# Attention masks in a two-layer decoder trunk: from bf16 matmuls into the score banks to an add inside the row-maximum instruction

## The chip, the cores and the metric

The kernel runs on one core of one Trainium2 chip. The time is in device microseconds (us), from the first to the last instruction of one execution as the device counts it; three runs of the kernel before gave a median of 985.11 us (984.95 to 986.36). Everything else below is read from one further execution that the hardware profiler recorded. The engines are TensorE (PE for its matmuls, PEld for its weight loads), VectorE (DVE), ScalarE (ACT), GpSimd (POOL) and the transfer queues.

## The reference

A layer has three attention branches over 256 tokens of width 1024, merged by gates, then a feed-forward part and a per-layer gate; there are two layers. What matters here is the attention:

```python
def masked_softmax(scores, mask):
    p = jax.nn.softmax(jnp.where(mask, scores, NEG_INF), axis=-1)
    return jnp.where(mask, p, 0.0)
# A: selected blocks and a window, both causal for 256 tokens, gated per head
# B: window of 128 keys (a band), with a learned sink per head:
sink = jnp.broadcast_to(sinks...)
p = jax.nn.softmax(jnp.concatenate([s, sink], axis=-1), axis=-1)[..., :-1]
# C: causal, latent attention, 8 heads of 96
```

Each branch has 8 heads. A also has a branch over 15 compressed keys, whose mask the change leaves as it is.

## The kernel before, in words

**Weights.** All weights are streamed once from HBM in chunks of two 128-row tiles by 512 columns. ScalarE rounds a chunk to its upper part (`wh`) and VectorE subtracts to get the lower part (`wl`). `lin` (line 316) multiplies 256 tokens by a weight matrix as three products of parts into a bank of PSUM, one bank per 128 tokens; the tile name of these banks is `lin`. Four raw chunks and six split chunks fit.

**Units of attention.** A unit is one bank of scores: 128 query rows, 512 columns. For the first 128 tokens (t = 0) a bank holds four row groups of 128 keys, for the second (t = 1) two of 256 keys. A layer has 24 such units: C has 2 with t = 0 and 4 with t = 1, A has 4 (`sw`, t = 0) and 8 (`sel` and `win`, t = 1), B has 2 and 4. Two units over compressed keys (`cmp`) come besides. Over two layers there are 48 units, 16 with four groups and 32 with two.

**The steps of a unit.** `qk` (line 859) first writes the mask into the bank by one bf16 matmul of the identity (`identb`) with `masks` (line 874): 512 columns for t = 0 and for B, else only the upper 256. The score matmuls then add to it (line 886; 4 to 8 of them). VectorE takes the negated maxima of the rows in one instruction (line 891, `negm`). For B three small instructions follow, which bring in the sink (lines 895 to 897). `ex` (line 899) has ScalarE take the exponential of each group, out of PSUM, with `negm` as the bias and with the row sum; `nrm` (line 912) inverts the sums on VectorE and scales `p`; `tr` (line 926) transposes `p` on TensorE and ScalarE copies the result (`pT`); `pvm` (line 938) multiplies with the values into a bank `pv`; after the last unit of a branch and t, `fin` (line 965) splits the output into `oT`. The tile `p` (three buffers, shared with a few other tiles) is taken in `ex`.

**The order.** Each engine runs its instructions in the order in which they are written. The class `Plan` (line 68) keeps an estimate of each engine's time from shapes alone; every step is queued with the time at which its operands are expected and is written between the matmuls of `lin` when the estimate of TensorE's time passes it (`tick`, line 139, after every three matmuls). A new unit is written (`hook`, line 848) when its inputs are there, fewer than two units wait for their exponential, and the estimate of TensorE's time is at least `SPACE` = 4.4 past that of the last unit. Where the main stream needs a result (`branch`, line 1093: branch C's products `wc0` need both of C's `oT`, `wb0` needs B's), `until` (line 151) writes all that is still queued up to it first.

**Once.** `setup_masks` (line 397) makes the bf16 identity, the rounded identity and the bf16 masks on VectorE. The arithmetic of the inverse roots (`newton`) is a chain of small instructions on POOL.

Of the kernel before, what the change touches and what calls it, by code (L numbers as in the profile page):

```python
# [10 lines left out]
BF16 = mybir.dt.bfloat16  # L11
I32 = mybir.dt.int32
AF = mybir.ActivationFunctionType
ALU = mybir.AluOpType
# [12 lines left out]
# The weight stream of a layer, in the order of use: name, k-tiles, columns, k-tiles of a chunk.  # L27
# [29 lines left out]
# columns of the constants, in three parts  # L57
# [3 lines left out]
# columns of a layer's small parameters  # L61
# [6 lines left out]
class Plan:  # L68
    """An estimate of when each engine's work ends, from shapes alone. Each engine runs its instructions in
    the order of emission, so a step that waits for another engine is put between the main stream's matmuls  # L70
    at the place where its operands are expected."""
# [19 lines left out]
    def clear(self, key, bufs):  # L91
        """Emit what still reads the slot's tile."""
        h = self.slots.setdefault(key, [])
        if len(h) >= bufs:
            for n in range(100):
                held = [x for x in self.q if h[-bufs] in x[3]]
                if not held:
                    break
                x = min(held, key=lambda x: x[:2])
                self.q.remove(x)  # L100
                was, self.busy = self.busy, True
                x[2]()
                self.busy = was
# [26 lines left out]
    def push(self, aps, fn, more=0.2, holds=()):  # L130
        """Emit fn when aps are expected; it reads the tiles of aps and holds."""
        self.n += 1
        self.q.append((max(self.at(*aps) + more, self.now), self.n, fn, {a.tensor.name for a in (*aps, *holds)}))
# [37 lines left out]
class Engine:  # L171
    """An engine whose instructions are entered into the plan."""
# [37 lines left out]
def build(tc, wst, xin, pin, posn, cst, lpar, fnorm, out):  # L210
# [39 lines left out]
    def upper(i):  # L250
        """Chunk i's upper parts."""
        for j in sorted(late):
            if j <= i - RAWB:
                late[j]()
        load_to(i + 1)
        off, kk, c = CHUNKS[i]
        r = raws.pop(i)
        hi = sb([P, 1024], F32R, name="wh", bufs=HLB, p=wp)
        lo = sb([P, 1024], F32R, name="wl", bufs=HLB, p=wp)
        w = kk * c  # L260
        S.copy(out=hi[:, :w], in_=r[:, :w])
        hls[i] = (hi, lo)

        def rest():
            late.pop(i)
            V.tensor_tensor(out=lo[:, :w], in0=r[:, :w], in1=hi[:, :w].bitcast(F32), op=ALU.subtract)
            load_to(i + 1 + RAWB)
        late[i] = rest

    def feed():  # L270
        """Split the next chunks where the engines have time."""
# [44 lines left out]
    def lin(l, name, nk, lhs, evac, blocks=None, wait=0.0, halves=False):  # L316
        """psum[tok, cols] = sum over k of lhs(t, k) x weights, three products of float32r parts."""
# [68 lines left out]
    identb = sb([P, P], BF16, name="identb")  # L386
    identr = sb([P, P], F32R, name="identr")
    masks = sb([P, 2, P], BF16, name="masks")
# [8 lines left out]
    def setup_masks():  # L397
        V.tensor_copy(out=identb, in_=ident)
        V.tensor_copy(out=identr, in_=ident)
        W.push([mload], lambda: V.tensor_copy(out=masks, in_=mload))  # L400
# [59 lines left out]
    def newton(ssq, n, tag, G=G):  # L460
        """(ssq + eps) ** -0.5 for [128, n]; a second term of ssq may be added."""
# [20 lines left out]
    def split_evac(src_ps, n, hi, lo, then, gain=None):  # L482
        """PSUM [128, n, 128] (times a gain per partition and n) -> parts."""
# [14 lines left out]
    def finish(t, r):  # L498
        """The final norm: x * gain lies in xf."""
# [11 lines left out]
    class Norm:  # L511
        """RMSNorm of x: transposed parts of x * gain; the inverse root goes into the products' outputs."""
# [16 lines left out]
        def square(self, t, g, c=slice(0, 512), part=0):  # L529
            """The sum of squares over columns c of half g, divided by D; the last norm also takes x * gain."""  # L530
# [54 lines left out]
    def rope(src, n, h, tab, dst):  # L585
        """src [128, n, 2h] -> dst; tab [128, 4h] = cos cos sin sin."""
# [8 lines left out]
    def layer(l, nm, nxt):  # L595
# [9 lines left out]
        # slots of 8 KB that the layer's stages share  # L605
# [41 lines left out]
        dup = [[None, None], [None, None]]  # L647
        vS = [sb([P, 3, P], name=f"v{t}") for t in range(2)]
# [210 lines left out]
        def qk(u):  # L859
# [5 lines left out]
            if t == 0:  # L865
                m = masks[:, 1:2, :].to_broadcast([P, 4, P])
                o = b.rearrange("p (a b) -> p a b", a=4)
            elif kind == "b":
                m = masks[:, None, :, :].to_broadcast([P, 2, 2, P])
                o = b.rearrange("p (c a b) -> p c a b", c=2, a=2)  # L870
            else:
                m = masks[:, 1:2, :].to_broadcast([P, 2, P])
                o = b.rearrange("p (c a b) -> p c a b", c=2, a=2)[:, :, 1, :]
            T.matmul(out=o, lhsT=identb, rhs=m, start=True, stop=True)
            for n, j in enumerate(js):
# [9 lines left out]
                for rk in rks:  # L885
                    T.matmul(out=b[:, n * w:(n + 1) * w], lhsT=lq, rhs=rk, start=False, stop=True,
                             skip_group_check=True)
            hs = slice(4 * c + js[0], 4 * c + js[0] + nh)
            b3 = b.rearrange("p (a b) -> p a b", a=ng)
            negm = small(4, "negm", 3)[:, :ng]  # L890
            V.tensor_reduce(out=negm, in_=b3, axis=AXX, op=ALU.max, negate=True)
            if v == "B":
                sk = lp[:, L_SINK:L_SINK + 8][:, hs]
                ns = small(4, "ns", 3)[:, :nh]
                V.tensor_scalar(out=ns, in0=sk, scalar1=-1.0, scalar2=None, op0=ALU.mult)
                V.tensor_tensor(out=negm, in0=negm, in1=ns, op=ALU.min)
                V.tensor_tensor(out=ns, in0=sk, in1=negm, op=ALU.add)

            def ex():
                p = sb([P, 512], name="p", bufs=3)  # L900
                state["open"] -= 1
                sm = small(4, "sm", 3)[:, :ng]
                for h in range(ng):
                    S.activation(out=p[:, h * nk:(h + 1) * nk], in_=b[:, h * nk:(h + 1) * nk], func=AF.Exp,
                                 bias=negm[:, h:h + 1], scale=1.0, accum_out=sm[:, h:h + 1])
# [70 lines left out]
            W.push([ns if v == "B" else negm], ex, 0.2, [b, negm])  # L976

        def qk_cmp(u):
# [18 lines left out]
            def nrm():  # L997
                V.tensor_reduce(out=m, in_=s, axis=AXX, op=ALU.add)
                V.reciprocal(out=m, in_=m)
                # gates lie as (c, j), the heads here as (j, c)  # L1000
# [266 lines left out]
    def warm(n):  # L1267
        """Keep the tensor engine's clock up until the first data are there."""
        for _ in range(n):
            nc.tensor.matmul(out=wps, lhsT=wrm[:, 0:P], rhs=wrm, start=True, stop=True)  # L1270
# [72 lines left out]
def host_layout(inputs):  # L1343
    """Weights in the order of use, chunk by chunk; small parameters along partitions."""
# [87 lines left out]
```

## Time and profile before

| | |
|---|---|
| median of three runs | 985.11 us |
| profiled execution, first to last instruction | 984.9 us |
| PE, busy | 967.0 us, 4915 matmuls |
| PEld, busy | 786.1 us |
| DVE, busy | 669.2 us, 1070 instructions |
| ACT, busy | 556.2 us, 1013 instructions |
| POOL, busy | 105.4 us, 224 instructions |

The page gives the span of the profiled execution and no other time of it; the median of the runs is 0.2 us above that span. Matmuls overlap in the records, because each is shown until its result is there; what one costs is read from the distance of two starts, and the same holds for two VectorE instructions in a row.

### The profile page before, as it was taken

To read this page: it belongs to the slowest core of one execution; us is meant where nothing else is said; L and a number is where in the kernel's file an instruction comes from. 1 tells how busy PE (TensorE), PEld (TensorE's weight loads), DVE (VectorE), ACT (ScalarE), POOL (GpSimd) and SP (SyncE) were. 2 spreads that over 40 slices of the span, in tenths; PEclk is the share of its full clock that TensorE was granted. 3 is DMA by queue.
4 is the path that set the end of the run, shared out by engine and by line. 5 is a ranking of instruction groups with operands and counts; after the bars stand their busy time and mean duration, and the time that the engine had idled before them with its cause. 6 is when DMAs were issued, how large, how long until landed. Compare 5 with 4: busy or idle time off the path is not lost.

```text
span 984.9 us, 13708 instructions
## 1 busy us (share of the span) xinstructions
PE 967.0 (98%) x4915; PEld 786.1 (80%) x4915; DVE 669.2 (68%) x1070; ACT 556.2 (56%) x1013; POOL 105.4 (11%) x224
## 2 busy tenths in 40 slices
PE   8899999999999999999999999999999999999996
PEld 5688887777888888888878898877778888888885
DVE  4687688658776666645767868876786766565555
ACT  5567766665555444543556686666655544444443
POOL 6610000000030000000444000000001200000032
PEclk9999999999999999999999999999999999999999
DMA  7445624434455555555454654343344555555551
GB/s 260 161 158 195 220 93 148 149 108 138 168 182 184 191 190 187 176 184 195 149 177 146 197 200 160 115 164 128 129 142 159 195 191 188 186 180 192 176 167 43
DMA packets 46596, 164.29 MB, mean 167 GB/s; under 512 B 5504, under 2 KB 5760, under 8 KB 46528
## 3 DMA queue, kind: packets, MB, share of 16 engines
q1 hardware_dynamic: 45648, 161.80, 48.7%
q0 software_dynamic: 448, 1.30, 0.4%
q8 instruction: 39, 0.64, 0.3%
q10 hardware_dynamic: 432, 0.32, 0.1%
q14 instruction: 29, 0.24, 0.1%
HBM read 162.35 MB, written 1.05 MB: 166 GB/s over the span
## 4 chain that ended last, share of the span: by engine, by line
PE 93%; POOL 3%; DVE 1%; issue 1%; ACT 1%; ACTq 0%; POOLq 0%; DVEq 0%
PE lin L206 78%; PE tr L206 6%; PE sc L206 5%; PE pv L206 3%; PE hidps L206 2%; POOL n1a L206 0%; POOL n0a L206 0%; POOL ang L206 0%; POOL kq L206 0%; ACT wh L206 0%; POOL kp L206 0%; DVE um L206 0%; DVE wl L206 0%; POOL n0y L206 0%; POOL n0v L206 0%
## 5 line engine op out<-in xcount | busy, mean ns | idle before, releaser
L206 PE MATMUL lin<-wh,hT 128*128 128x512 f32 (+2 forms) x1600 | 516.9, 392 | 1.5 <-DVE hT L206 0.8
L206 DVE TENSOR_TENSOR wl<-raw,wh 128x1024 fp32r<-128x1024 f32 (+2 forms) x308 | 369.1, 1209 | 94.6 <-ACT wh L206 89.5
L206 ACT CAST wh<-raw 128x1024 fp32r<-128x1024 f32 (+2 forms) x308 | 317.3, 1038 | 138.8 <-PE lin L206 135.7
L206 PEld LDWEIGHTS lin<-wh,hT 128*128 128x128 f32 x1600 | 297.9, 189 | 61.8 <-DVE hT L206 1.7
L206 PE MATMUL lin<-wl,hT 128*128 128x512 f32 (+2 forms) x800 | 308.1, 385 | 2.3 <-DVE wl L206 2.3
L206 PEld LDWEIGHTS lin<-wl,hT 128*128 128x128 f32 x800 | 151.1, 189 | 29.7 <-DVE wl L206 3.1
L206 PE MATMUL lin<-wh,hd 128*128 128x512 f32 x352 | 112.6, 397 | 0.0
L206 PEld LDWEIGHTS lin<-wh,hd 128*128 128x128 f32 x352 | 66.2, 188 | 15.2
L206 POOL TENSOR_SCALAR n0v<-ssq 128x1 f32<-128x1 f32 x7 | 2.5, 358 | 694.1 <-ACT junk L206 694.1
L206 PE MATMUL lin<-wl,hd 128*128 128x512 f32 x176 | 69.4, 394 | 0.0
L206 PE MATMUL lin<-wh,oT 128*128 128x512 f32 x192 | 64.7, 398 | 0.0
L206 ACT ACTIVATE th<-lin,rh 128x256 f32<-128x256 f32 (+1 forms) x52 | 26.3, 505 | 67.8 <-PE lin L206 67.7
L206 ACT ACTIVATE p<-sc,negm 128x256 f32<-128x256 f32 (+1 forms) x128 | 52.7, 427 | 2.7 <-DVE negm L206 2.7
L206 DVE SCALAR_TENSOR_TENSOR th<-th,lin 128x256 f32<-128x256 f32 x44 | 18.4, 418 | 50.6 <-ACT th L206 50.6
L206 DVE TENSOR_REDUCE negm<-sc 128x2 f32<-128x512 f32 (+1 forms) x48 | 33.0, 688 | 27.9 <-PE sc L206 27.5
L206 ACT COPY pT<-tr 128x512 f32<-128x512 f32 x48 | 28.1, 585 | 36.8 <-PE tr L206 36.5
L206 PEld LDWEIGHTS lin<-wh,oT 128*128 128x128 f32 x192 | 36.0, 188 | 7.9 <-issue 0.8
L206 PE MATMUL lin<-wh,mT 128*128 128x512 f32 x128 | 42.0, 399 | 0.0
L206 PEld LDWEIGHTS lin<-wl,hd 128*128 128x128 f32 x176 | 33.1, 188 | 7.5
L206 PE MATMUL lin<-wl,oT 128*128 128x512 f32 x96 | 37.6, 392 | 0.0
L206 ACT CAST hd<-tr 128x256 fp32r<-128x256 f32 x44 | 16.3, 370 | 33.8 <-PE tr L206 33.8
L206 DVE TENSOR_TENSOR p<-p,sm 128x512 f32<-128x512 f32 x48 | 33.2, 692 | 2.1
(226 smaller groups left out, 1073.3 us busy)
## 6 DMA issues: line engine op xcount, KB each, us to landing
raw<-wst SPq DMA_DIRECT2D x296, 512.0 KB, 4.0
raw<-wst SPq DMA_DIRECT2D x8, 312.0 KB, 2.8
raw<-wst SPq DMA_DIRECT2D x4, 384.0 KB, 3.0
x<-xin SPq DMA_DIRECT2D x4, 256.0 KB, 6.0
w<-lpar POOLq DMA_DIRECT2D x2, 256.0 KB, 3.2
pr<-pin POOLq DMA_DIRECT2D x2, 256.0 KB, 3.3
fn<-fnorm SPq DMA_DIRECT2D x1, 512.0 KB, 3.1
out<-xf SPq DMA_DIRECT2D x2, 256.0 KB, 2.1
```

The source lines that it names most:

```text
L206: return fn(*a, **k)
```

## The change

- The mask matmuls go, with `identb` and the bf16 masks. The first score matmul of a group now starts its part of the bank and the last one ends it.
- `masks` becomes float32, four blocks of 128 columns: band, causal, zeros, causal. A t = 0 unit takes the last block, a t = 1 unit of B the first two, the other t = 1 units the zeros and the causal block. GpSimd writes the zeros, ScalarE copies the others, in two instructions.
- The one row-maximum instruction of a unit becomes one `tensor_tensor_reduce` per group (four for t = 0, two for t = 1). It reads the scores from PSUM and the mask from SBUF, writes p = -(score + mask) to SBUF over the whole group, and puts the smallest of these and of a start value in `negm`. The start value is the negated sink for B, else 3e38.
- The negated sinks of a layer (`nsk`) are made once on GpSimd as the layer begins. Of B's three small VectorE instructions in each unit one is left.
- The exponential is taken in place from p in SBUF, with scale -1.0.
- `p` is now taken in `qk`, and the queue of the plan holds `p` where it held the bank.

The diff, cut to these places (it also drops comments):

```diff
-    identb = sb([P, P], BF16, name="identb")
     identr = sb([P, P], F32R, name="identr")
-    masks = sb([P, 2, P], BF16, name="masks")
+    masks = sb([P, 4, P], name="masks")
...
     def setup_masks():
-        V.tensor_copy(out=identb, in_=ident)
         V.tensor_copy(out=identr, in_=ident)
-        W.push([mload], lambda: V.tensor_copy(out=masks, in_=mload))
+        G.memset(masks[:, 2:3, :], 0.0)
+        W.push([mload], lambda: S.copy(out=masks[:, 0:2, :], in_=mload))
+        W.push([mload], lambda: S.copy(out=masks[:, 3:4, :], in_=mload[:, 1:2, :]))
...
+        nsk = small(8, "nsk", 1)
+        G.tensor_scalar(out=nsk, in0=lp[:, L_SINK:L_SINK + 8], scalar1=-1.0, scalar2=None, op0=ALU.mult)
...
-            T.matmul(out=o, lhsT=identb, rhs=m, start=True, stop=True)
...
-                for rk in rks:
-                    T.matmul(out=b[:, n * w:(n + 1) * w], lhsT=lq, rhs=rk, start=False, stop=True,
-                             skip_group_check=True)
+                for i, rk in enumerate(rks):
+                    T.matmul(out=b[:, n * w:(n + 1) * w], lhsT=lq, rhs=rk, start=i == 0,
+                             stop=i == len(rks) - 1, skip_group_check=True)
...
-            V.tensor_reduce(out=negm, in_=b3, axis=AXX, op=ALU.max, negate=True)
+            m = masks[:, 3, :] if t == 0 else masks[:, 0:2, :] if kind == "b" else masks[:, 2:4, :]
+            p = sb([P, 512], name="p", bufs=3)
+            for h in range(ng):
+                r = slice(h * nk, (h + 1) * nk)
+                i1 = m if t == 0 else m.rearrange("p a b -> p (a b)")
+                V.tensor_tensor_reduce(out=p[:, r], in0=b[:, r], in1=i1, scale=-1.0,
+                                       scalar=nsk[:, hs][:, h:h + 1] if v == "B" else 3e38,
+                                       op0=ALU.add, op1=ALU.min, accum_out=negm[:, h:h + 1])
             if v == "B":
-                sk = lp[:, L_SINK:L_SINK + 8][:, hs]
                 ns = small(4, "ns", 3)[:, :nh]
-                V.tensor_scalar(out=ns, in0=sk, scalar1=-1.0, scalar2=None, op0=ALU.mult)
-                V.tensor_tensor(out=negm, in0=negm, in1=ns, op=ALU.min)
-                V.tensor_tensor(out=ns, in0=sk, in1=negm, op=ALU.add)
+                V.tensor_tensor(out=ns, in0=lp[:, L_SINK:L_SINK + 8][:, hs], in1=negm, op=ALU.add)
...
-                p = sb([P, 512], name="p", bufs=3)
...
-                    S.activation(out=p[:, h * nk:(h + 1) * nk], in_=b[:, h * nk:(h + 1) * nk], func=AF.Exp,
-                                 bias=negm[:, h:h + 1], scale=1.0, accum_out=sm[:, h:h + 1])
+                    S.activation(out=p[:, h * nk:(h + 1) * nk], in_=p[:, h * nk:(h + 1) * nk], func=AF.Exp,
+                                 bias=negm[:, h:h + 1], scale=-1.0, accum_out=sm[:, h:h + 1])
...
-            W.push([ns if v == "B" else negm], ex, 0.2, [b, negm])
+            W.push([ns if v == "B" else negm], ex, 0.2, [p, negm])
```

## Rows read from the trace of the kernel before

All instructions are written by helpers on line 206, so rows are told apart by their tiles.

**Rows 1.** The page: busy time of each engine with its share of the span and its instructions, and the shares of the chain that ended last by engine.

```profile
PE 967.0 (98%) x4915; PEld 786.1 (80%) x4915; DVE 669.2 (68%) x1070; ACT 556.2 (56%) x1013; POOL 105.4 (11%) x224
...
PE 93%; POOL 3%; DVE 1%; issue 1%; ACT 1%; ACTq 0%; POOLq 0%; DVEq 0%
```

**Rows 2.** Busy time in stretches: from and to, length, then PE, PEld, DVE, ACT and POOL busy with their instructions, granted clock, DMA share, GB/s. The first two are the attention of layer 0 and of layer 1, the third a part of the first.

```profile
101.00:240.00 139.00, 138.50 (x838) 111.22 (x838) 103.89 (x204) 91.33 (x230) 0.64 (x1) 1.00 0.42 141
582.00:719.00 137.00, 136.50 (x826) 109.95 (x825) 102.70 (x203) 89.94 (x228) 0.61 (x1) 1.00 0.41 141
...
140.00:160.00 20.00, 20.00 (x114) 16.12 (x114) 18.27 (x36) 13.65 (x46) 0.00 (x0) 1.00 0.33 111
```

**Rows 3.** Groups of instructions, shapes kept apart: the mask matmuls (count, then busy us, mean ns of one, idle before).

```profile
L206 PE MATMUL sc<-masks,identb 128*128 128x512 bf16 x24 | 9.3, 387 | 0.0
...
L206 PE MATMUL sc<-masks,identb 128*128 128x256 bf16 x24 | 6.7, 278 | 0.0
```

**Rows 4.** Timeline of PE at two units of C: start, length, instruction. A mask of 512 columns and the score matmul behind it, then one of 256 columns and the one behind it.

```profile
106.49 0.39 PE L206 MATMUL sc<-masks,identb 128*128 128x512 bf16 x1
106.72 1.06 PE L206 MATMUL sc<-kTC,qTC 96*128 96x128 f32 x8
...
111.60 0.27 PE L206 MATMUL sc<-masks,identb 128*128 128x256 bf16 x1
111.71 1.03 PE L206 MATMUL sc<-kTC,qTC 96*128 96x256 f32 x4
```

**Rows 5.** Groups by shape on DVE and ACT: the row maxima, the nearest two-operand instructions of 256 and 128 columns, the read of ScalarE's accumulator, and a ScalarE cast of 256 columns out of PSUM and out of SBUF.

```profile
L206 DVE TENSOR_REDUCE negm<-sc 128x2 f32<-128x512 f32 x32 | 22.0, 688 | 16.2 <-PE sc L206 15.9
...
L206 DVE TENSOR_REDUCE negm<-sc 128x4 f32<-128x512 f32 x16 | 11.0, 686 | 11.6 <-PE sc L206 11.6
...
L206 DVE TENSOR_TENSOR hd<-tr,hd 128x256 fp32r<-128x256 f32 x44 | 18.6, 422 | 10.0 <-ACT hd L206 10.0
...
L206 DVE TENSOR_TENSOR cs_s<-cs_s,cs_m 128x128 f32<-128x128 f32 x8 | 2.3, 292 | 0.3
...
L206 ACT ACTIVATION_READ_ACCUMULATOR p<-sc,negm 128x1 f32 x128 | 26.9, 210 | 0.0
...
L206 ACT CAST hd<-tr 128x256 fp32r<-128x256 f32 x44 | 16.3, 370 | 33.8 <-PE tr L206 33.8
...
L206 ACT CAST q<-kall 128x256 fp32r<-128x256 f32 x16 | 5.7, 405 | 15.3 <-DVE kall L206 15.3
```

**Rows 6.** Timeline, instructions that stand back to back on one engine: two of 256 columns and a row maximum on DVE, two small ones of a B unit on DVE, and two exponentials of 128 columns on ACT (the accumulator's read between them is left out).

```profile
142.32 0.76 DVE L206 TENSOR_TENSOR kall<-ra,rb 128x256 f32<-128x256 f32 x2
142.99 0.68 DVE L206 TENSOR_REDUCE negm<-sc 128x4 f32<-128x512 f32 x1
143.59 2.35 DVE L206 TENSOR_TENSOR wl<-raw,wh 128x1024 fp32r<-128x1024 f32 x2
...
144.74 0.36 ACT L206 ACTIVATE p<-sc,negm 128x128 f32<-128x128 f32 x1
...
145.09 0.35 ACT L206 ACTIVATE p<-sc,negm 128x128 f32<-128x128 f32 x1
...
204.06 0.16 DVE L206 TENSOR_SCALAR ns<-lp 128x4 f32<-128x4 f32 x1
204.25 0.16 DVE L206 TENSOR_TENSOR negm<-negm,ns 128x4 f32<-128x4 f32 x1
```

**Rows 7.** Timeline of layer 0 where branch C ends: the last unit's scaling on DVE, its transposes, the split of C's output, and the first matmul of `wc0`.

```profile
134.35 0.69 DVE L206 TENSOR_TENSOR p<-p,sm 128x512 f32<-128x512 f32 x1
...
135.40 0.60 PE L206 MATMUL tr<-con,p 128*128 128x128 f32 x4
...
140.40 0.69 DVE L206 TENSOR_TENSOR oT<-pv,oT 128x512 fp32r<-128x512 f32 x1 [1.78 <-ACT oT L206]
...
141.23 0.39 PE L206 MATMUL lin<-wh,oT 128*128 128x512 f32 x1
```

**Rows 8.** The same where branch B ends: the last unit's mask, its scaling, transposes, the cast of the output, and the matmuls in which `wa1` ends and `wb0` begins (the second of the two).

```profile
230.29 0.39 PE L206 MATMUL sc<-masks,identb 128*128 128x512 bf16 x1
...
236.03 0.69 DVE L206 TENSOR_TENSOR p<-p,sm 128x512 f32<-128x512 f32 x1
...
237.49 0.60 PE L206 MATMUL tr<-con,p 128*128 128x128 f32 x4
...
240.54 0.59 ACT L206 CAST oT<-pv 128x512 fp32r<-128x512 f32 x1 [0.67 <-PE pv L206]
...
241.00 0.62 PE L206 MATMUL lin<-wh,oT 128*128 128x512 f32 x2
```

**Rows 9.** Timeline of PE: the masks of two units of A that follow one another.

```profile
186.68 0.27 PE L206 MATMUL sc<-masks,identb 128*128 128x256 bf16 x1
...
191.91 0.28 PE L206 MATMUL sc<-masks,identb 128*128 128x256 bf16 x1
```

**Rows 10.** Timeline of the start: the making of the identity and the masks on DVE, PE's wait for a lower part behind them, and ScalarE's wait before its second gate.

```profile
25.16 0.22 DVE L206 CAST identb<-con 128x128 bf16<-128x128 f32 x1
...
25.43 0.29 DVE L206 CAST masks<-mload 128x256 bf16<-128x256 f32 x1
...
26.91 0.50 PE L206 MATMUL lin<-wl,hT 128*128 128x512 f32 x1 [1.12 <-DVE wl L206]
...
31.48 0.69 ACT L206 ACTIVATE gateC<-lin,rh 128x512 f32<-128x512 f32 x1 [3.51 <-POOL rh L206]
```

More of the change, by code (lines that the diff above doesn't have):

```diff
@@ L864, in qk @@
             ng = 512 // nk
[L865 to L873, printed above, removed]
-            T.matmul(out=o, lhsT=identb, rhs=m, start=True, stop=True)
             for n, j in enumerate(js):
@@ L884, in qk @@
                 w = 512 // nh
-                for rk in rks:
-                    T.matmul(out=b[:, n * w:(n + 1) * w], lhsT=lq, rhs=rk, start=False, stop=True,
-                             skip_group_check=True)
+                for i, rk in enumerate(rks):
+                    T.matmul(out=b[:, n * w:(n + 1) * w], lhsT=lq, rhs=rk, start=i == 0,
+                             stop=i == len(rks) - 1, skip_group_check=True)
             hs = slice(4 * c + js[0], 4 * c + js[0] + nh)
-            b3 = b.rearrange("p (a b) -> p a b", a=ng)
             negm = small(4, "negm", 3)[:, :ng]
-            V.tensor_reduce(out=negm, in_=b3, axis=AXX, op=ALU.max, negate=True)
+            m = masks[:, 3, :] if t == 0 else masks[:, 0:2, :] if kind == "b" else masks[:, 2:4, :]
[6 more added lines that the diff above has]
+                                       op0=ALU.add, op1=ALU.min, accum_out=negm[:, h:h + 1])
             if v == "B":
-                sk = lp[:, L_SINK:L_SINK + 8][:, hs]
                 ns = small(4, "ns", 3)[:, :nh]
-                V.tensor_scalar(out=ns, in0=sk, scalar1=-1.0, scalar2=None, op0=ALU.mult)
-                V.tensor_tensor(out=negm, in0=negm, in1=ns, op=ALU.min)
-                V.tensor_tensor(out=ns, in0=sk, in1=negm, op=ALU.add)
+                V.tensor_tensor(out=ns, in0=lp[:, L_SINK:L_SINK + 8][:, hs], in1=negm, op=ALU.add)
             def ex():
-                p = sb([P, 512], name="p", bufs=3)
                 state["open"] -= 1
```

## The prediction

> **What bounds the kernel now.** I read the page's busy times and the chain that ended last, then busy time by stretches for the two attention stages, then the distances of starts in the timeline. TensorE is busy for 98% of the span and makes 93% of the chain [rows 1]. In layer 0's attention it is busy for 138.5 of 139 us, in layer 1's for 136.5 of 137 [rows 2]: it waits for nobody there, so in these stages each us that it is spared would be worth a us, as long as the engines that feed it keep up. VectorE, which gets the work, is busy for 103.9 of 139 us, 75%, but unevenly: 18.27 of 20 us where branch A's first units meet the products of C [rows 2]. There it is as good as full. ScalarE has 91 of 139.
>
> **Removed from TensorE.** A mask of 512 columns holds the next matmul off by 106.72 - 106.49 = 0.23 us, one of 256 columns by 111.71 - 111.60 = 0.11 [rows 4]. There are 24 of each [rows 3]: 24 x 0.23 + 24 x 0.11 = 5.5 + 2.6 = 8.2 us, 4.1 a layer, all of it on the path. The mean durations of 387 and 278 ns in the groups [rows 3] hold the latency too and are not the cost. The granted clock is 1.00 of the full 2.4 GHz in these stretches, with TensorE at work throughout [rows 2], and what replaces the masks is other matmuls, so I let it stay.
>
> **Moved to VectorE.** The maximum takes 0.69 us [rows 5], and the instruction behind it starts 143.59 - 142.99 = 0.60 later [rows 6]; that is the slot. No row shows an add with a reduction, so I bound it. From below it is a plain two-operand instruction: two of 256 columns take 142.99 - 142.32 = 0.67, a slot of 0.335 each [rows 6]; for 128 columns 0.29 [rows 5] less the same 0.09 of overlap, 0.20. From above it is the full duration plus a separate read of the accumulator as long as ScalarE's, 0.21: 0.42 + 0.21 = 0.63 and 0.29 + 0.21 = 0.50 [rows 5]. On ScalarE the read costs less than its duration: exponentials of 128 columns stand 145.09 - 144.74 = 0.35 apart, read included [rows 6]. That is the nearest row for an instruction with an accumulator, so I take 0.12 on top of the plain slot: 0.455 and 0.32.
> A unit with two groups then costs VectorE 2 x 0.455 - 0.60 = +0.31 us, one with four 4 x 0.32 - 0.60 = +0.68. B's two dropped small instructions had 204.25 - 204.06 = 0.19 each [rows 6], -0.38 a unit. Sum over 32, 16 and 12 units: 9.9 + 10.9 - 4.6 = +16 us. From below: 32 x 0.07 + 16 x 0.20 - 4.6 = +1 us. From above: 32 x 0.66 + 16 x 1.40 - 4.6 = +39 us. Less than nothing is possible for B's units alone, where 2 x 0.335 stands against 0.60 + 0.38.
>
> The Trainium skill, "VectorE: DVE Perf Modes", section "Two Vector instructions with no wait between them", says that an instruction which also writes out its accumulator is really two, the main one and a read. It speaks against this change, as it would make 128 more instructions; no trace here shows it on VectorE, and it has no price. If it holds the upper reckoning is the closer one, if it doesn't the lower.
>
> **Where it meets the path.** A layer has three stretches.
> First, up to the first matmul of C's products. The last scaling of C's `p` starts at 134.35 and its transposes at 135.40, 0.36 us after it ends; C's output is split at 140.40 and `wc0` starts at 141.23, just behind its end [rows 7]. There is no slack, and this chain is held by VectorE, which is full here [rows 2]. So the masks taken out ahead of it (2 x 0.23 + 4 x 0.11 for C, 0.23 for A's first: 1.1 us) bring nothing, and C's last two units may cost up to 2 x 0.31. I take half, +0.3 us.
> Second, the other three units of A with four groups: 3 x 0.68 = 2.0 us more for a full VectorE. The weights are split several chunks ahead and the transposes follow their scalings with some room, so I count no stall; if that cover is gone, it costs 2 us less the 0.7 of their masks.
> Third, A's later units and B's, where VectorE has room. The masks here are 8 x 0.11 + 6 x 0.23 = 2.3 us, with the three above 3.0 us. But the units are paced, not packed: the two masks stand 5.23 us apart [rows 9], about SPACE's 4.4 of the plan's time and one round of three matmuls. With less work of its own per unit, the plan puts more of the main stream between units, so the main stream is further on when B's last unit comes. And B's end has no slack either: the mask of the last unit is at 230.29, the cast of the output ends at 241.13, and `wb0` begins with the second matmul of the pair at 241.00, some 0.23 later [rows 8]. What can close up is 237.49 - 236.72 = 0.8 us between scaling and transposes, and about as much behind them [rows 8]. Of the 3.0 us I therefore let 1.6 arrive.
> A layer gains 1.6 - 0.3 = 1.3 us, two layers 2.6.
>
> **The rest.** At the start VectorE loses two casts that stand ahead of a lower part for which TensorE waits 1.12 us [rows 10]; with 0.22 and 0.29 us of duration they are worth some 0.3 us at most. ScalarE gets two copies instead, for which I take 0.2 of this back: it waits 3.51 us before its second gate [rows 10], which covers them unless they stand ahead of a chunk's upper part; then they cost up to 0.7. POOL's zeros and the negated sinks are 3 small instructions on an engine that is 11% busy [rows 1]; ahead of an inverse root they would cost some 0.3 us in a layer. No DMA moves.
> The exponential reads SBUF instead of PSUM: a cast of 256 columns takes 405 ns from there and 370 from PSUM [rows 5], so 128 x 0.035 = 4.5 us more for ScalarE. It has room [rows 2], and only the last unit's 0.07 is in B's end. Nothing is gained where the bank comes free earlier, since TensorE doesn't wait for it. Taking `p` in `qk` adds a wait: VectorE's add, and all behind it, waits for the transposes of three tiles back. Three units are 3 x 5.2 = 15.7 us [rows 9], and a unit's `p` lives about 7 us, from 230.29 to 237.49 [rows 8], so I cost it at nothing; if other tiles of that slot crowd it, it is a stall of a us or two.
>
> **Sum.** 984.9 - 2.6 - 0.1 = 982.2 us of span; the median of the runs stands 0.2 above the span, so 982.3.
>
> **The rivals.**
> All of it arrives: 984.9 - 8.2 gives 976.9 as a median. For it: TensorE bounds the attention [rows 1, 2], and the plan knows of the removed matmuls and can order around them. Against it: both ends of branches without slack [rows 7, 8].
> The pace takes it all: the units keep their distance, the main stream arrives early and waits at `wc0` and `wb0`: 985. For it: the distance [rows 9] is the plan's and not the engine's. Against it: the chain of B's last unit can close up by 0.8 us and more.
> VectorE becomes the bound, slower: with the upper price a layer's C units 3 to 6 (4 x 0.66 = 2.6 us) and A's four first ones (4 x 1.40 = 5.6 us) put 8 us on VectorE between 112 and 157 us, where the row of 140 to 160 leaves it 1.7 us idle in 20 [rows 2], say 3.5 in that stretch. TensorE is held by the other 4.5 us, less the 1.6 that the last stretch still gives: 2 x 2.9 = +6, 991. It decides from the point where the extra work there passes the idle time by more than 1.6 us, at about 0.53 and 0.41 for the two sizes, midway between my price and the upper one. For it: the four instructions where one was, and VectorE's order, in which the lower parts of the weights stand behind them. Against it: the plan counts VectorE's new instructions too, if too low, and moves their readers back.
>
> **How the numbers follow.** All arrives 0.15 (976 to 979). Part arrives, the forecast, 0.40 (979 to 983.7). The pace takes it all 0.22 (983.7 to 986.5). VectorE bounds 0.23 (986.5 to 993). The forecast's own range is 979 to 983.7. Two microseconds, 0.2%, is what a measurement here can tell from no change. Faster, below 983.1: the first case, most of the second: 0.15 + 0.36 = 0.51. Slower, above 987.1: 0.22. The rest, 0.27, is the same. The range for 8 in 10 takes in most of the first case and half of the last: 977 to 989.
>
> **What would show it.** The mask matmuls are gone and TensorE's busy time falls by about what the chain gains, while waits of TensorE for `p`'s scalings or for `oT` appear at `wc0` and `wb0`. The adds stand 0.3 and 0.45 us apart, VectorE's busy time rises by 16 us, and by 3 us within 140 to 160. A loss would show TensorE waiting for VectorE between 120 and 165 us of layer 0 and at the same place of layer 1, a full gain no such wait. I am wrong if the adds cost less than 0.30 or more than 0.55 at 256 columns, if the plan's new order puts a branch's end elsewhere, or if the difference arises outside the attention.

## The result, and the profile after

The changed kernel takes 999.16 us (median of four runs, 999.0 to 999.38), the kernel before on the same chip 985.65 (984.95 to 986.36): ratio 1.0136 [1.0124, 1.0148], 13.5 us slower. The prediction was 982.3, in a range of 977 to 989. The profiled execution has a span of 997.2 us where the kernel before had 984.9.

The page after: busy times, and the shares of the chain that ended last by engine.

```profile
PE 969.2 (97%) x4867; PEld 783.1 (79%) x4867; DVE 674.0 (68%) x1252; ACT 561.8 (56%) x1015; POOL 107.1 (11%) x227
...
PE 88%; DVE 6%; POOL 2%; ACT 2%; issue 1%; ACTq 0%; DVEq 0%; POOLq 0%
```

Against [rows 1] TensorE has 48 matmuls fewer and is still 2.2 us longer busy: some of its work has run slower. VectorE, which took the masks over, is only 4.8 us longer busy, yet its share of the chain rises from 1% to 6%. Both have to be explained.

The waits of TensorE, longest in total first: total us, times, longest.

```profile
PE tr L206 <- DVE p L206: 7.6, 4, 3.6
PE tr L206 <- DVE w L206: 2.3, 2, 1.1
```

The kernel before has neither row. The two long waits for `p` stand where B ends, one a layer; those for `w`, one a layer too, are in the chain that makes A's compressed keys, at 124.90 us in layer 0.

The same stretches as in [rows 2]: from and to, length, PE, PEld, DVE, ACT and POOL busy with their instructions, granted clock, DMA share, GB/s.

```profile
101.00:240.00 139.00, 133.77 (x794) 107.89 (x794) 107.09 (x298) 92.85 (x226) 0.64 (x1) 1.00 0.42 138
582.00:719.00 137.00, 135.00 (x807) 109.91 (x806) 102.92 (x284) 94.10 (x226) 0.61 (x1) 1.00 0.43 143
140.00:160.00 20.00, 20.00 (x112) 16.21 (x111) 18.70 (x54) 15.05 (x45) 0.00 (x0) 1.00 0.42 137
```

From 140 to 160, where VectorE was feared to be full, it is 18.70 us busy against 18.27 and TensorE waits for nobody. Groups by shape, to set against the maxima of [rows 5]: count, busy us, mean ns of one, idle before.

```profile
L206 DVE CUSTOM_DVE_ANT_0 p<-sc,masks 128x256 f32<-128x256 f32 x48 | 18.4, 422 | 18.9 <-PE sc L206 18.6
L206 DVE CUSTOM_DVE_ANT_0 p<-sc,masks 128x128 f32<-128x128 f32 x48 | 11.1, 287 | 9.4 <-PE sc L206 9.4
L206 DVE DVE_READ_ACCUMULATOR2_ANT negm<- 128x1 f32 x128 | 10.7, 84 | 0.0
L206 DVE CUSTOM_DVE_ANT_0 p<-sc,masks,nsk 128x256 f32<-128x256 f32 x16 | 7.1, 481 | 3.2 <-PE sc L206 3.2
```

And the end of B in layer 0, which answers to [rows 8]. First VectorE, then ScalarE, then TensorE.

```profile
233.73 0.69 DVE L206 TENSOR_TENSOR p<-p,sm 128x512 f32<-128x512 f32 x1
234.34 0.48 DVE L206 CUSTOM_DVE_ANT_0 p<-sc,masks,nsk 128x256 f32<-128x256 f32 x1
...
234.74 0.48 DVE L206 CUSTOM_DVE_ANT_0 p<-sc,masks,nsk 128x256 f32<-128x256 f32 x1
...
235.34 2.36 DVE L206 TENSOR_TENSOR wl<-raw,wh 128x1024 fp32r<-128x1024 f32 x2
237.61 0.68 DVE L206 SCALAR_TENSOR_TENSOR tm<-gateA,lin 128x512 f32<-128x512 f32 x1
238.33 0.69 DVE L206 TENSOR_TENSOR mg<-mg,tm 128x512 f32<-128x512 f32 x1
...
239.32 0.69 DVE L206 TENSOR_TENSOR p<-p,sm 128x512 f32<-128x512 f32 x1
```

```profile
236.27 0.49 ACT L206 ACTIVATE p<-p,negm 128x256 f32<-128x256 f32 x1
...
236.76 0.19 ACT L206 ACTIVATE es<-ns 128x2 f32<-128x2 f32 x1
```

```profile
231.89 0.72 PE L206 MATMUL sc<-khB,qhl 128*128 128x256 f32 x4
...
236.20 0.40 PE L206 MATMUL lin<-wh,oT 128*128 128x512 f32 x1
240.16 0.63 PE L206 MATMUL tr<-con,p 128*128 128x128 f32 x4 [3.56 <-DVE p L206]
```

ScalarE's last exponential of this unit's scores began at 236.27, and all its sums were there at 236.76 + 0.19 = 236.95; but on VectorE two lower parts, a gate product and a sum stand ahead of the scaling, which starts 2.4 us later. TensorE has nothing left to do from 236.6 on. Before, 21 of the main stream's matmuls lay between the last scores and these transposes; now 9 do.

In the kernel before VectorE had work ahead of this scaling as well, one lower part less, and ScalarE's sums came there at 234.93 + 0.21 = 235.14, 0.9 us before the scaling at 236.03 [rows 8]:

```profile
233.18 1.23 DVE L206 TENSOR_TENSOR wl<-raw,wh 128x1024 fp32r<-128x1024 f32 x1
...
234.32 0.68 DVE L206 SCALAR_TENSOR_TENSOR tm<-gateA,lin 128x512 f32<-128x512 f32 x1
...
235.04 0.69 DVE L206 TENSOR_TENSOR mg<-mg,tm 128x512 f32<-128x512 f32 x1
```

```profile
234.93 0.21 ACT L206 ACTIVATE es<-ns 128x2 f32<-128x2 f32 x1
```

How the time differs from before, counted from the end of C's projections at 100 us (executions of every kernel differ by a step of 1.5 to 2 us ahead of that, so spans alone mislead by as much). The kernels e7, e13 and e16 are told of below.

| difference to before, us, at the first | after | e7 | e13 | e16 |
|---|---|---|---|---|
| `mg` of C's products, layer 0 | +1.6 | -0.7 | +1.6 | +1.6 |
| product with `gateB`, layer 0 | +5.2 | -3.7 | +5.6 | +1.9 |
| last `h` of layer 0 | +6.6 | -3.6 | +6.0 | +1.5 |
| `mg` of C's products, layer 1 | +9.4 | -3.8 | +8.2 | +3.4 |
| product with `gateB`, layer 1 | +12.9 | -6.8 | +11.1 | +3.7 |

### The profile page after: what moved, and what is told of

The parts are those of the page before. It is cut to its first block, busy times and chain, and to the rows that moved or that the text cites. A ratio compares the mean times of both kernels' runs of the same rounds, so it can differ in the third digit from the quotient of the medians.

```text
span 997.2 us, 13792 instructions
## 1 busy us (share of the span) xinstructions
PE 969.2 (97%) x4867; PEld 783.1 (79%) x4867; DVE 674.0 (68%) x1252; ACT 561.8 (56%) x1015; POOL 107.1 (11%) x227
## 4 chain that ended last, share of the span: by engine, by line
PE 88%; DVE 6%; POOL 2%; ACT 2%; issue 1%; ACTq 0%; DVEq 0%; POOLq 0%
PE lin L206 75%; PE tr L206 6%; PE sc L206 3%; PE pv L206 3%; DVE wl L206 2%; PE hidps L206 2%; DVE p L206 1%; ACT wh L206 1%; POOL kp L206 0%; DVE mg L206 0%; POOL n0a L206 0%; DVE tm L206 0%; POOL ang L206 0%; POOL n1a L206 0%; DVE um L206 0%
## 5 line engine op out<-in xcount | busy, mean ns | idle before, releaser
L206 PE MATMUL lin<-wh,oT 128*128 128x512 f32 x192 | 68.2, 410 | 0.0
L206 ACT ACTIVATE p<-p,negm 128x256 f32<-128x256 f32 (+1 forms) x128 | 56.8, 447 | 3.8 <-DVE negm L206 3.8
L206 DVE CUSTOM_DVE_ANT_0 p<-sc,masks 128x128 f32<-128x128 f32 (+1 forms) x96 | 29.6, 355 | 28.3 <-PE sc L206 28.0
L206 PE MATMUL tr<-con,p 128*128 128x128 f32 x192 | 29.3, 275 | 8.1 <-DVE p L206 7.6
```

What stands on the lines that cost most here:

```text
L206: return fn(*a, **k)
```

## The experiments

**Work or order? (e1, e2)** The plan decides the order from the instructions that it is told of. e1 does the new work and tells the plan of the old; e2 does the old work and tells it of the new. TensorE's order is then that of before, masks aside, in e1, and the changed one in e2.

```diff
# e1, on the changed kernel (the setup, the dropped small instructions and the queue's tiles likewise)
+            W.op("T", (512 if t == 0 or kind == "b" else 256) * 0.4173e-3, [b.tensor.name], [masks.tensor.name])
...
-                V.tensor_tensor_reduce(out=p[:, r], in0=b[:, r], in1=i1, scale=-1.0,
+                nc.vector.tensor_tensor_reduce(out=p[:, r], in0=b[:, r], in1=i1, scale=-1.0,
...
+            W.op("V", 0.08 + 512 * 1.08e-3, [negm.tensor.name], [b.tensor.name])
...
# e2, on the kernel before (the setup and the dropped small instructions likewise)
-            T.matmul(out=o, lhsT=identb, rhs=m, start=True, stop=True)
+            nc.tensor.matmul(out=o, lhsT=identb, rhs=m, start=True, stop=True)
...
-            V.tensor_reduce(out=negm, in_=b3, axis=AXX, op=ALU.max, negate=True)
+            p = sb([P, 512], name="p", bufs=3)
+            nc.vector.tensor_reduce(out=negm, in_=b3, axis=AXX, op=ALU.max, negate=True)
+            for _ in range(ng):
+                W.op("V", 0.08 + nk * 1.08e-3, [p.tensor.name, negm.tensor.name], [b.tensor.name])
```

> The changed kernel's work (masks added by VectorE, no mask matmuls), but the plan is charged as before: each unit enters a mask matmul that is not issued, and one tensor_reduce in place of its additions, so TensorE's instructions stand in the order of before, less the 48. Theory 1 (the loss is the new order: the plan's shorter units move B's last ones to a later place in the main stream): the loss is gone and most of the 8.2 us of masks arrive, 977 to 982 us; if the addresses in SBUF cost the feed-forward its 1 us per layer, 979 to 984. Rival (VectorE's additions themselves are late at B's end, wherever its units stand): TensorE still waits some 3 us at each layer's join of B, 994 to 1000 us.

> The kernel of before (48 mask matmuls, tensor_reduce from PSUM), but the plan is charged as in the changed kernel: masks free on TensorE, each unit's additions entered on VectorE, so that TensorE's instructions stand in the changed order with the masks among them. Theory 1 (order): it loses as the changed kernel does, plus the masks it still issues: 997 to 1007 us, with a wait of TensorE for p's scaling of 2 us or more at each join of B. Rival (the additions): the order is harmless with the old work, 985 to 988 us.

e1: 983.44 us, ratio 0.9972 [0.9963, 0.9982]. e2: 1002.68, ratio 1.0168 [1.0149, 1.0186]. In e2 TensorE waits for the same scalings, though no addition is in the kernel:

```profile
PE tr L206 <- DVE p L206: 7.2, 2, 3.6
```

So the loss is the order's, whichever engine adds the masks. But e1 brought 2.7 us and not 8.2.

**The addresses (e3, e5, e11, e12).** In the changed kernel the feed-forward, which the change does not touch, is 1.1 us longer in each layer: from the first to the last write of `h`, 290.49 to 411.73 us before (121.24) and 293.79 to 416.11 after (122.32):

```profile
290.49 0.48 DVE L206 SCALAR_TENSOR_TENSOR h<-th,rh,lin 128x256 f32<-128x256 f32 x1
...
411.73 0.48 DVE L206 SCALAR_TENSOR_TENSOR h<-th,rh,lin 128x256 f32<-128x256 f32 x1
```

```profile
293.79 0.48 DVE L206 SCALAR_TENSOR_TENSOR h<-th,rh,lin 128x256 f32<-128x256 f32 x1
...
416.11 0.48 DVE L206 SCALAR_TENSOR_TENSOR h<-th,rh,lin 128x256 f32<-128x256 f32 x1
```

The kernel's tiles lie one behind the other. `identb` (256 bytes per partition) is gone, `masks` has 2048 bytes for 512, so all tiles behind move by 1280 bytes; `nsk` adds 32 for those behind it, among them the split weights, while a part of the tiles for the activations' parts (`hT`, `oT`, `hd`), which serve about half of the products, lies ahead of it. These kernels are the kernel before with unused tiles, each written once on GpSimd; nothing else changes.

```diff
# e3: a tile of 1280 bytes behind masks
+    pad = sb([P, 320], name="pad")
# e5: 32 bytes where the changed kernel has nsk, ahead of the weights, behind the first of the activations' parts
+        npad = small(8, "npad", 1)
# e11: 32 bytes ahead of both
+    hpad = sb([P, 8], name="hpad")
# e12: hpad and npad, so that the first of the activations' parts move by 32 bytes and the weights by 64
```

> The kernel of before with an unused tile of 1280 bytes per partition behind the masks, so that the later tiles' addresses in SBUF move by as much as in the changed kernel; every engine's order is that of before. Theory that the feed-forward's slower matmuls (0.233 in place of 0.231 us on the average, some 1 us per layer) come of the addresses: 987 to 988.5 us. Rival (they come of something else, the clock among it): 985.0 to 986.3 us.

> The kernel of before with one unused tile of 32 bytes per partition where the changed kernel has its negated sinks, so that every tile behind it, the weights' split parts among them, lies 32 bytes further, as in the changed kernel (where the shift of these tiles is 1312 bytes, that is 20 times 64 and 32; the pad of 1280 left the remainder as it was). Theory (the slower matmuls come of the remainder of the weights' addresses by 64 bytes): the feed-forward, first to last write of h, takes 122.3 us per layer in place of 121.23, and the whole 2.5 to 4 us more than before, 987.5 to 989.5. Rival (they come of the changed work): 121.23 and 985 to 986.3 us.

> The kernel of before with an unused tile of 32 bytes ahead of the tables, so that the activations' parts (hT, oT, hd: the products' stationary side) and the weights' parts (the moving side) both lie 32 bytes further, at a remainder of 0 by 64. Theory (the remainder of the moving side decides by itself): h's stretch at 122.3 us per layer and 989 to 991. Rival (the two sides must not lie differently): 121.2 and 984.5 to 986.5.

> As the run before this one, with a second unused 32 bytes ahead of the values' tile, so that only the activations' parts move to a remainder of 0 by 64 and the weights' parts keep 32. Theory (the moving side decides): 121.2 us per layer and 984.5 to 986.5. Rival (the two sides must not lie differently): 122.3 and 989 to 991.

| | first activations, weights moved by (bytes) | time | ratio | `h`, layer 0 |
|---|---|---|---|---|
| e3 | 1280, 1280 | 984.83 | 0.9998 [0.9988, 1.0007] | 121.23 |
| e5 | 0, 32 | 990.75 | 1.0055 [1.0040, 1.0070] | 122.30 |
| e11 | 32, 32 | 984.90 | 0.9997 [0.9987, 1.0007] | 121.27 |
| e12 | 32, 64 | 990.66 | 1.0050 [1.0033, 1.0066] | 122.34 |

The first and the last write of `h` in e11, then in e12:

```profile
288.69 0.48 DVE L206 SCALAR_TENSOR_TENSOR h<-th,rh,lin 128x256 f32<-128x256 f32 x1
...
409.96 0.48 DVE L206 SCALAR_TENSOR_TENSOR h<-th,rh,lin 128x256 f32<-128x256 f32 x1
```

```profile
290.79 0.48 DVE L206 SCALAR_TENSOR_TENSOR h<-th,rh,lin 128x256 f32<-128x256 f32 x1
...
413.13 0.48 DVE L206 SCALAR_TENSOR_TENSOR h<-th,rh,lin 128x256 f32<-128x256 f32 x1
```

My theory that the weights' own place decides fell: e11 moves them as e5 does and loses nothing, e12 leaves them at their old remainder by 64 and loses. What costs time is to move the two sides of a product, stationary and moving, apart by 32 bytes of 64. e1's missing time is this. e5's whole loss is 4.3 us of slower products all through (its trace against e3's, behind the start) and, in the median, the step at the start.

Only a part of the products loses by it. In the feed-forward the stationary side is, twelve products at a time, an `hT` tile ahead of the pad or one behind it, which moves along with the weights. In the kernel before nine products take 309.07 - 307.03 = 2.04 us with the tile ahead and 312.09 - 309.99 = 2.10 with the one behind; in e5 they take 309.60 - 307.50 = 2.10 with the tile ahead. First the kernel before, then e5:

```profile
307.03 0.62 PE L206 MATMUL lin<-wh,hT 128*128 128x512 f32 x2
...
309.07 0.39 PE L206 MATMUL lin<-wh,hT 128*128 128x512 f32 x1
...
309.99 0.63 PE L206 MATMUL lin<-wh,hT 128*128 128x512 f32 x2
...
312.09 0.62 PE L206 MATMUL lin<-wh,hT 128*128 128x512 f32 x2
```

```profile
307.50 0.63 PE L206 MATMUL lin<-wh,hT 128*128 128x512 f32 x2
...
309.60 0.39 PE L206 MATMUL lin<-wh,hT 128*128 128x512 f32 x1
```

Over the whole kernel the mean distance of two starts is 0.2297 us with tiles ahead and 0.2334 with tiles behind in the kernel before, 0.2331 and 0.2332 in e5, and 0.2305 and 0.2330 in e7 below, where the two sides are moved apart by 64. So the shift by 32 takes from about half of the products an advantage that the other half never had, although its two sides have the same remainder by 64 in the kernel before. What else the faster value takes, no run here shows.

**The work alone, the order alone (e7, e6, e13).** With a tile of 64 bytes for the negated sinks both sides keep their remainder by 64.

```diff
# e7: e1 with this line; e13: the changed kernel with it alone
-        nsk = small(8, "nsk", 1)
+        nsk = small(16, "nsk", 1)[:, 0:8]
# e4: the changed kernel with this one alone; e6: with both
-    SPACE = 4.4
+    SPACE = 4.2
```

> The changed kernel's work in the order of before, with the same 64-byte tile. Theory (addresses, and the masks' matmuls lie on the path of TensorE): the gain over the kernel before is what the attention gave, some 6 of the 8.2 us: 979 to 981. Rival (the first such run's missing 5 us were lost to the additions): 983 as without it.

> The changed kernel as it is, its order too, with only the 64-byte tile for the negated sinks. If the two causes add, the loss without the address part is the order's alone: 994 to 996 us, TensorE still waiting 3.6 us at each join of B. Rival (the two hang together, the slow matmuls make the join late): 985 us or less.

e7: 978.64 us, 0.9933 [0.9918, 0.9948]. e13: 996.69, 1.0107 [1.0092, 1.0122]. Both have the same work, addresses and start; their spans are 976.1 and 994.3. The order alone costs 18.2 us, and without it the masks bring 985 x 0.67% = 6.6 of their 8.2. The table shows where: in layer 0 2.3 us up to C's products and 7.0 more up to B's, in layer 1 2.4 and 5.9. A small part is not understood: e13's feed-forward takes 121.54 us in each layer where e7's takes 121.28.

**Wait and clock (e8).** Behind the wait the granted clock falls from full to half; the changed kernel in steps of 2 us:

```profile
240.00:242.00 2.00, 1.69 (x10) 0.91 (x11) 1.15 (x2) 0.58 (x1) 0.00 (x0) 0.89 0.53 203
242.00:244.00 2.00, 2.00 (x8) 0.95 (x5) 0.00 (x0) 0.49 (x1) 0.00 (x0) 0.50 0.82 258
244.00:246.00 2.00, 2.00 (x8) 1.63 (x7) 1.82 (x2) 0.09 (x1) 0.00 (x0) 0.76 0.01 4
```

0.50 is 1.2 of 2.4 GHz. The shortfall is 2 x (0.11 + 0.50 + 0.24) = 1.7 us of full clock. e8, on the changed kernel, fills the wait with products on a constant tile, which are overwritten.

```diff
+                if v == "B" and js[-1] == 3 and c == 1 and t == 1:
+                    for _ in range(32):
+                        nc.tensor.matmul(out=tb[:, 0:256], lhsT=fil[:, 0:P], rhs=fil, start=True, stop=True)
```

> The changed kernel, with 32 matmuls of 256 bf16 columns (0.11 us each) on a constant tile put ahead of the transposes that wait at each layer's join of B; their products are overwritten. The order of all else is the changed kernel's, and so are the addresses by 64 bytes. If the clock that falls after the wait of 3.6 us is a part of the loss, TensorE stays at full clock and 1.5 to 4 us of the 13.5 come back: 995 to 997.7. Rival (the wait alone is the loss; the clock falls beside it at no cost): 999 to 1000.5.

996.95 us, 1.0119 [1.0104, 1.0134]. The clock stays at 1.00, and from the end of C's projections to the first product with `gateB` layer 0 takes 1.5 us less than in the changed kernel; layer 1 gains the same 1.5 over its own stretch. The clock is 3 us of the loss; the wait, 3.6 a layer, is more.

**VectorE's order (e16).** In e13 the last scaling of a layer's B is queued earlier; TensorE keeps its order at this join. Behind it the plan then also moves the transposes of `mg` by a few places.

```diff
-                W.push([p, sm] + [es] * (es is not None), lambda: nrm(p, sm, es))
+                W.push([p, sm] + [es] * (es is not None), lambda: nrm(p, sm, es),
+                       -2.5 if v == "B" and t == 1 and c == 1 and js[-1] == 3 else 0.2)
```

> The changed kernel with the 64-byte tile, and the last scaling of a layer's B queued 2.7 us earlier in the plan, so that on VectorE it stands ahead of one lower part, one gate product and one sum of the merge (1.22 + 0.68 + 0.69 us by their records) and behind one lower part. TensorE's order round that join is the changed kernel's, with its 9 matmuls between the last scores and their transposes. Theory (what stands ahead of the scaling on VectorE makes the wait): the scaling starts some 2 us earlier, as soon as ScalarE's sums are there; TensorE's wait at each join of B is 1.2 to 2 us in place of 3.6, with 0 to 1.5 us of clock saved beside it, and the whole 2 x 1.9 to 2 x 3.3 us below the same kernel without it (996.7): 990 to 993. Rival (the scaling is late because the scores and their additions are, its place on VectorE matters little): the wait stays above 3 us, 995.5 to 997.

989.25 us, 1.0034 [1.0020, 1.0049], 7.4 below e13. VectorE, then the transposes:

```profile
236.78 1.22 DVE L206 TENSOR_TENSOR wl<-raw,wh 128x1024 fp32r<-128x1024 f32 x1
238.43 0.16 DVE L206 TENSOR_TENSOR sm<-sm,es 128x2 f32<-128x2 f32 x1 [0.43 <-ACT es L206]
...
238.82 0.69 DVE L206 TENSOR_TENSOR p<-p,sm 128x512 f32<-128x512 f32 x1
```

```profile
239.66 0.63 PE L206 MATMUL tr<-con,p 128*128 128x128 f32 x4 [1.62 <-DVE p L206]
```

The scaling now waits for ScalarE and not behind VectorE's other work. TensorE's wait is 1.62 us and the granted clock stays at 1.00. By the first product with `gateB` layer 0 has gained 3.7 us on e13 (the table), wait and clock together; another 0.8 comes behind it, up to the last `h`, where the moved transposes stand, so the whole is a little more than I had reckoned. What is left of the wait I put down to the place of the unit, with 9 matmuls over its chain; no run changes that alone.

**The spacing (e4, e6, e9, e10, e14, e15).** Is there a better one, or does every new order lose?

> The changed kernel with the units paced 4.2 us of planned TensorE time apart in place of 4.4. Theory 1 (order): B's last units stand some 2 to 3 us earlier in the main stream, about what the uncounted masks had moved them, so that the joins of B recover: 978 to 990 us. Rival (the additions make the chain late however it is paced): 995 to 1001 us.

> The changed kernel with its units 4.2 us apart and the negated sinks in a tile of 64 bytes in place of 32, so that the weights' parts stand at the same remainder by 64 bytes as in the kernel before. Theory (addresses): the feed-forward is back at 121.2 us per layer, and the whole 2.5 to 4 us below the run with 4.2 alone: 979 to 980.5. Rival (the changed work): 122.3 us and 982.5 to 983.5.

> The kernel of before, nothing changed but the spacing of the units, 4.2 us of planned TensorE time in place of 4.4: the control for the two runs with 4.2. If the gain of those is the change's (masks off TensorE), this one stays near 984.9, between 983.5 and 986.5. Rival (a shorter spacing is worth as much to the old kernel): 978 to 982 us.

> The changed kernel with the 64-byte tile and units 4.0 us apart. If only the cliff at 4.4 (B's last units behind the end of the work that covers them) cost time, a still shorter spacing brings nothing more: 978 to 980.5, as with 4.2. Rival (each step of the spacing closes up the chain further): 975 to 977.5.

> The changed kernel with the 64-byte tile and the units 4.3 us apart. In its order 30 matmuls of the main stream stand between the scores of B's last unit and the transposes of its p (21 in the kernel before, 9 in the changed kernel, 18 with 4.2). Theory (that cover decides, at B's join): no wait for p there, 977 to 981 us. Rival (4.2 was a lucky value and any other loses): 985 to 1000.

> The same with 4.5 us; 30 matmuls stand between the last scores and their transposes here too. Theory (cover at B's join): no wait there, 977 to 982 us, unless another join has taken its place, which its page would show as a new wait of TensorE of 2 us or more. Rival (the longer the spacing, the later B and the larger the loss): above 995.

| | kernel, spacing | time | ratio |
|---|---|---|---|
| e10 | changed, 64 bytes, 4.0 | 988.66 | 1.0034 [1.0020, 1.0047] |
| e6 | changed, 64 bytes, 4.2 | 978.89 | 0.9934 [0.9917, 0.9950] |
| e14 | changed, 64 bytes, 4.3 | 995.19 | 1.0097 [1.0081, 1.0113] |
| e13 | changed, 64 bytes, 4.4 | 996.69 | 1.0107 [1.0092, 1.0122] |
| e15 | changed, 64 bytes, 4.5 | 994.26 | 1.0085 [1.0068, 1.0102] |
| e4 | changed, 32 bytes, 4.2 | 982.95 | 0.9978 [0.9968, 0.9988] |
| e9 | before, 4.2 | 989.43 | 1.0044 [1.0029, 1.0059] |

e9 and e10 came out where neither side had them, and e14 and e15 miss my theory: with 30 matmuls over B's last chain its long wait is gone, and another takes its place. The first row is e14's, where C ends (e15 waits 1.90 us there); the second e10's, in the compressed keys.

```profile
139.87 0.30 PE L206 MATMUL tr<-con,p 128*128 128x128 f32 x1 [1.89 <-DVE p L206]
```

```profile
130.76 0.92 PE L206 MATMUL tr<-w 128*128 128x128 f32 x4 [2.37 <-DVE w L206]
```

The spacing has no trend; each value is another order, and an order is good only if it clears three joins at once: compressed keys, end of C, end of B. The orders of before at 4.4 and of the changed kernel at 4.2 do; those of e10, e13, e14 and e15 miss one. To clear them is not enough: e9 loses 2 us a layer with no wait above 0.73 us behind the start, and I leave its cause open.

e7 and e6 beat both kernels, by 0.67% [0.52, 0.82] and 0.66% [0.50, 0.83].

## Why the prediction was wrong

**What bounds the kernel, and the masks' worth.** Right. With order and addresses held, e7 gains 6.6 of the 8.2 us that I reckoned. The rival "all of it arrives", 976.9, is nearly what the work alone is worth.

**VectorE's price.** The new instructions cost less than I took. Two additions of 256 columns start 110.63 - 110.28 = 0.35 us apart, with the sink 234.74 - 234.34 = 0.40; I had 0.455. Of 128 columns 0.21, where I had 0.32:

```profile
105.73 0.29 DVE L206 CUSTOM_DVE_ANT_0 p<-sc,masks 128x128 f32<-128x128 f32 x1
105.94 0.08 DVE L206 DVE_READ_ACCUMULATOR2_ANT negm<- 128x1 f32 x1
105.94 0.29 DVE L206 CUSTOM_DVE_ANT_0 p<-sc,masks 128x128 f32<-128x128 f32 x1
...
110.28 0.42 DVE L206 CUSTOM_DVE_ANT_0 p<-sc,masks 128x256 f32<-128x256 f32 x1 [0.65 <-PE sc L206]
...
110.63 0.42 DVE L206 CUSTOM_DVE_ANT_0 p<-sc,masks 128x256 f32<-128x256 f32 x1
```

The read of the accumulator is a second instruction, but it starts together with the next addition, and the slot is hardly longer than the 0.335 of a plain instruction [rows 6]. That there are two is what the Trainium skill, "VectorE: DVE Perf Modes", section "Two Vector instructions with no wait between them", says, and the trace agrees (128 reads beside 128 additions). VectorE's busy time rose by 4.8 us, not 16; the lower bound of +1 was the closer end. The rival "VectorE becomes the bound" came nearest in time, 991, but that is luck: its price (0.53 and 0.41) was not reached, and no wait arose between 140 and 160.

**First stretch, +0.3.** With the old order it gains 0.7; the changed kernel loses 1.6 there, the compressed keys' wait of 1.15 us among it. The step had the new order in no term.

**Third stretch, -1.6: the step that failed.** I saw that B's end has no slack [rows 8], that the units are paced by the plan [rows 9], and that the plan would put the units at other places of the main stream. From that I took that a late B gives back at most what the masks save, "the pace takes it all", 985. That is no lower bound: an order can give back more than was saved. The changed order left 9 matmuls over a chain that had 21, and put four large instructions of VectorE ahead of the last scaling where three had stood, so that it came 2.4 us behind ScalarE's sums and not 0.9. That cost 3.6 us of wait and 1.5 of clock per layer. Of all I took from the rows, that the chain "can close up by 0.8 us and more" was most at fault: it is a statement on hardware waits in the old order, and in a new one the chain on VectorE has other work inside. With the old order the stretch brings 3.0 us, all of its masks' worth, where I let 1.6 arrive.

**The clock, "I let it stay".** It stayed while TensorE stayed busy; I didn't carry the loss of clock behind a new wait into any rival.

**Outside the attention.** Nothing was foreseen. The 32 bytes of `nsk` slowed the products: 2.9 us between the spans of e13 and the changed kernel. I had named a difference that "arises outside the attention" and an order that "puts a branch's end elsewhere" as what would prove me wrong; both happened.

**ScalarE and the start.** Exponentials of 128 columns stand 145.27 - 144.88 = 0.39 us apart where they stood 0.35 apart [rows 6], which is the 0.035 expected, and TensorE's new waits, for `p` and `w`, are for VectorE:

```profile
144.88 0.39 ACT L206 ACTIVATE p<-p,negm 128x128 f32<-128x128 f32 x1
145.27 0.39 ACT L206 ACTIVATE p<-p,negm 128x128 f32<-128x128 f32 x1
```

By the end of C's projections e13 is within 0.1 us of e3, which started like it, against -0.1 expected.

**The sum.** As measured: work -6.6, order +18.2, addresses +2.9, together +14.5. The traces give 14.5 too, counted from the end of C's projections to the end; the medians give 13.5, the difference being within the step at the start. The forecast's last step was loose as well: 982.2 and 0.2 make 982.4, and the 0.2 compares the median with the span of another execution. An execution's time is 1.8 us above its own span (999.0 and 997.2), so the execution profiled before, whose time is not on record, took some 986.7 by my estimate.

## What to carry to other kernels

When instructions are placed by estimates, a change of one price moves everything placed behind it: run the new work in the old order and the old work in the new order before either is believed, and look for what stands ahead of the critical instruction on its own engine. Where joins have no slack, price a rival in which the reordering misses one, with the wait and the clock behind it. After adding or removing tiles, compare a stretch that the change doesn't touch; if it moved, look at the addresses.

## What the runs showed of the hardware

- Products of 128 x 128 by 512 took 0.2297 us from start to start with some stationary tiles and 0.2334 with others in the same kernel. When the two SBUF operands of the faster half were moved apart by 32 bytes of 64, these took 0.2331 (the feed-forward 122.3 us in place of 121.2, 0.9%); moved alike by 32, or apart by 64, they stayed at 0.2305 or below. The slower half, with equal remainders by 64 too, stayed at 0.233.
- After a wait of 3.56 us TensorE ran for part of the next 6 us at 1.2 GHz, 1.5 us lost; after one of 1.62 us the clock stayed at 2.4.
- An addition with a reduction costs a slot of 0.35 us for 256 columns from PSUM and SBUF, hardly more than the 0.335 of a plain two-operand instruction out of SBUF [rows 6]; with a start value by pointer it is 0.40.
